# Loads for a half's end issued during its last gate and up block, and VectorE adds to y in the last row line

## The chip, the cores and the metric

The kernel runs on one core of one Trainium2 chip. The metric is device time in microseconds of one execution, as the median over runs. The engines of the core are TensorE (PE; its weight loads stand apart as PEld), VectorE (DVE), ScalarE (ACT), GpSimd (POOL) and SyncE (SP), and 16 DMA engines that move data between HBM and the on-chip memory. SP issues nearly all loads, in the order of its queue; POOL issues the few transfers that add while they move.

## What is computed

One layer of a hybrid encoder on 256 tokens of width 2048, in float32. It is a feed-forward half step, a mixing stage (attention and a Fourier branch), and another feed-forward half step:

```python
def _swiglu(x, w_gate, w_up, w_down):
    return (jax.nn.silu(x @ w_gate) * (x @ w_up)) @ w_down

def _macaron_ffn(x, pre_g, w_gate, w_up, w_down, post_g):
    return x + MACARON_WEIGHT * _rms_norm(_swiglu(_rms_norm(x, pre_g), w_gate, w_up, w_down), post_g)
...
        h = _macaron_ffn(h, ffn1_pre_g[l], ffn1_w_gate[l], ffn1_w_up[l], ffn1_w_down[l], ffn1_post_g[l])
        h = _gated_mixers(h, mix_pre_g[l], w_in[l], b_gate[l], q_norm_g[l], k_norm_g[l],
                          w_attn_o[l], w_fourier[l], w_out[l], mix_post_g[l], rope)
        h = _macaron_ffn(h, ffn2_pre_g[l], ffn2_w_gate[l], ffn2_w_up[l], ffn2_w_down[l], ffn2_post_g[l])
```

The hidden width of a feed-forward half is 5632. The change touches the two feed-forward halves alone.

## The kernel before

**Number format.** Each float32 factor is split into a high part (line 104, ScalarE) and a low part (line 105, VectorE), and a product is three matmuls: high by high, high by low, low by high (lines 110 to 112). TensorE's work is therefore fixed by the shapes, and every weight that is loaded costs one ScalarE and one VectorE instruction before TensorE can use it.

**A half (`ffn`, line 703).** The hidden width is cut into 11 blocks of 512. For each block, gate and up products are formed (a 2048-deep sum), silu and multiplication give the block of hidden values, these are transposed on TensorE, and the block's rows of the down matrix are multiplied and added to `y`, which has 256 tokens (two tiles of 128, `t` = 0 and 1) by 2048 columns (four column blocks `cb` of 512). The first two gate and up blocks are done plainly; the nine that follow run through a software pipeline:

- `swiglu` (line 558) is one gate and up block. Its depth is cut into eight pairs of 128-deep pieces. Pairs 0, 1, 2, 4, 5 and 6 use a seven-product scheme (`seven`, 21 matmuls a pair), pairs 3 and 7 the plain one (`plain`, 24 matmuls a pair). For the scheme VectorE first forms sums of weights (line 582). Even pairs load 1 MB at once (`raw4`), the others 512 KB pieces (`raw`).
- `row_line` (line 658) is one row block of the down product: four column blocks of 24 matmuls, with two weight pieces each. At the start of its last column block (`ahead`) the next block's hidden values are transposed.
- `Line` (line 525) is the queue that holds both together: a step's weights are loaded and split when it is fed, and its matmuls come when it is popped, up to `RING` = 6 steps later, or 8 (`RING + RING_B8`) where `turn["more"]` is set. With `turn["more"]` every fourth split goes into a place of the pool `b8` (line 512) and not into the ring.
- The steps' order on TensorE, ScalarE and VectorE is the order of the code (`manual_schedule`, line 735). The order on SP and POOL, and of what stands outside such a section, is a planner's, which works with modelled times.

The loop at line 736 runs f from 2 to 11; its f-th turn does row block f - 2, then gate and up block f. So in the order of TensorE the last gate and up block (f = 10) is followed by row block 9 (f = 11), and row block 10 follows in `last_rows`.

**The pool `b8`** has 12 places of 1 MB. In the pipeline two hold `y`; six hold the *left factors*: the normalized input in the forms that the two schemes need, made once a half (`Forms`, line 443) and put into three rooms of two places each, in the order of the pairs. The first room holds pairs 0, 1 and the first two forms of pair 2, the second the rest of pair 2 and pairs 3 and 4, the third pairs 5, 6 and half of pair 7. The other four places turn over among `raw4` and the splits of `turn["more"]`.

**How y is added up.** Of each row block, column blocks 2 and 3 (`onto`) start from y: ScalarE copies y into PSUM (line 681), TensorE adds on top, ScalarE copies back (line 691). Column blocks 0 and 1 start from zero: ScalarE copies the result into a buffer `part` (line 694), and a DMA issued from POOL adds that to y while it moves it (line 695).

**The end of a half (`last_rows`, line 261).** Row block 10 runs token tile by token tile. For each, ScalarE first copies y's column block into PSUM (`row_part`, line 219), TensorE adds the product, and the squares for the norm (line 379) and the rest of the norm follow. This needs `h` (the residual, two places of b8, 1 MB a tile) and the norms' gains as broadcast rows (`gpost`, and in the first half `gpre` for the stage behind it; 1 MB each). `tail` loads them: line 795 for the first half, where h is the input x, and line 1225 for the second, where it comes from a spill in DRAM and there is only one gain. It is called when TensorE's order reaches column block 1 of row block 9 (line 744), though SP may issue the loads whenever their places are free.

Of the kernel before, what the change touches and what calls it, by code (L numbers as in the profile page):

```python
# [15 lines left out]
ALU = mybir.AluOpType  # L16
# [33 lines left out]
PLAIN = 2  # L50
# [8 lines left out]
def encoder_layer(  # L59
# [495 lines left out]
            while self.queue:  # L555
                self.next()

    def swiglu(line, forms, w, hs):


        ps, begun, x = {}, set(), {}

        def mul(n, a, b, last=False):
            if n not in ps:
                ps[n] = ptr.tile([P, NB], F32, tag="tr", name="pc") if n in ("p5", "p7", "p1") else                     pmm.tile([P, NB], F32, tag="mm", name="pc")
            mm3(ps[n][:], *a, *b, n not in begun, last)
            begun.add(n)

        def raw(pair, i):
            return raw_piece(w[pair // 2], pair % 2 * 2 + i)  # L570

        def plain(pair, i, *then, hold=False):
            def use(b):
                for t in range(NT):
                    for j in range(2):
                        k = 2 * pair + j
                        mul("gu"[i] + str(t), forms.plain[k][t], b[j], k == KD - 1)

            line.feed(lambda: ring(raw(pair, i)[:]), use, *then, hold=hold)

        def minus(out, a, b):
            V.tensor_tensor(out=out, in0=a, in1=b, op=ALU.subtract)  # L582

        def add(out, a, b):
            if out not in x:
                x[out] = work(out)
            V.tensor_tensor(out=x[out][:], in0=ps[a][:], in1=x[b][:], op=ALU.add)

        def copy():
            x["x1"] = work("x1")  # L590
            A.activation(x["x1"][:], ps["p1"][:], AF.Copy)

        def silu(t):
            g = x["x" + "13"[t]]
            A.activation(g[:], g[:], AF.Silu)

        def times(t):
            g, up = x["x" + "13"[t]], x["x" + "25"[t]]
            V.tensor_tensor(out=up[:], in0=up[:], in1=g[:], op=ALU.mult)
            hs.append(up)  # L600

        def seven(pair, between=None, *then):
            a11, a12, na22, s1, s2, s3, s4 = forms.seven[pair]
            end = pair == BY_SEVEN[-1]
            h = {}

            def first():
                t = chunk.tile([P, WP, NB], F32, tag=("ch_hi", "ch_lo")[BY_SEVEN.index(pair) % 2], name="t13")
                if turn["more"] and pair in RAW_B8:
                    four = big("raw4", F32, [P, 2 * WP, NB])  # L610
                    load(four[:], w[pair // 2].rearrange("p (i k c) -> p i k c", i=2, c=NB)[:, pair % 2])
                    ra, rb = four[:, 0:WP, :], four[:, WP:, :]
                    minus(t[:], four[:, 1:3, :], ra)
                else:
                    ra, rb = raw(pair, 0), raw(pair, 1)
                    minus(t[:, 0, :], ra[:, 1, :], ra[:, 0, :])
                    minus(t[:, 1, :], rb[:, 0, :], ra[:, 1, :])
                h.update(ra=ra, rb=rb, t=t)
                b = ring(rb[:])
                minus(ra[:, 1, :], rb[:, 0, :], t[:, 0, :])  # L620
                return b

            def second():
                b = ring(h["t"][:])
                minus(h["t"][:, 0, :], h["ra"][:, 1, :], h["rb"][:, 1, :])
                return b

            def two(n, a, m, b, last):
                def use(ws):
                    mul(n, a, ws[0], last)  # L630
                    mul(m, b, ws[1], last)
                return use

            line.feed(first, two("u0", s4, "g0", a12, False))
            line.feed(second, two("p5", s1, "p7", s3, end), hold=end)
            if between:
                between()
            line.feed(lambda: ring(h["ra"][:]), two("p1", a11, "p6", s2, end), *then[0:2], hold=end)
            line.feed(lambda: ring(h["t"][:, 0:1, :]), lambda ws: mul("g1", na22, ws[0]), *then[2:], hold=end)

        sums = [copy, lambda: add("x2", "p6", "x1"), lambda: add("x3", "p7", "x2"), lambda: add("x2", "p5", "x2"),
                lambda: add("x5", "p5", "x3")]
        gates = [lambda: add("x1", "g0", "x1"), lambda: add("x3", "g1", "x3"), lambda: silu(0), lambda: silu(1)]
        ups = [lambda: add("x2", "u0", "x2"), lambda: times(0), lambda: add("x5", "u1", "x5"), lambda: times(1)]
        for kg in range(KD // CK):
            a, b = 2 * kg, 2 * kg + 1
            if kg == KD // CK - 1:
                seven(a, None, *sums)
                plain(b, 0, *gates, hold=True)
                plain(b, 1, *ups)  # L650
            elif b in BY_SEVEN:
                seven(a)
                seven(b)
            else:
                seven(a, lambda: plain(b, 0))
                plain(b, 1)

    def row_line(line, ch, w, rb, y, first, ahead):

        rooms = {(0, 0): (ptr, "tr"), (1, 0): (ptr, "tr"), (1, 1): (ptr, "tr")} if not first else {}
        ps = {}

        def onto(cb):
            return cb >= ONTO and not first

        def place(cb, t):
            pool, tag = rooms.get((cb, t), (pmm, "mm"))
            ps[cb, t] = pool.tile([P, NB], F32, tag=tag, name="pr")  # L670

        def use(b, cb, i):
            if i == 0 and cb in ahead:
                ahead[cb]()
            for t in range(NT):
                if i == 0 and not onto(cb):
                    place(cb, t)
            if i == 1 and cb + 2 < D // NB and onto(cb + 2):
                for t in range(NT):
                    place(cb + 2, t)  # L680
                    A.activation(ps[cb + 2, t][:], cbs(y[t], cb + 2), AF.Copy)
            for t in range(NT):
                for j in range(WP):
                    k = i * WP + j
                    mm3(ps[cb, t][:], ch[0][:, k, t * P:(t + 1) * P], ch[1][:, k, t * P:(t + 1) * P], *b[j],
                        k == 0 and not onto(cb), k == CK - 1, onto(cb))

        def out(t, cb):
            dst = cbs(y[t], cb)
            if first or onto(cb):  # L690
                A.activation(dst, ps[cb, t][:], AF.Copy)
            else:
                part = work("part")
                A.activation(part[:], ps[cb, t][:], AF.Copy)
                nc.gpsimd.dma_start(dst, part[:], accum_op=ALU.add)

        for cb in range(D // NB):
            for i in range(CK // WP):
                line.feed(lambda i=i, cb=cb: ring(raw_piece(w[rb, cb], i)[:]),
                          lambda b, cb=cb, i=i: use(b, cb, i),  # L700
                          *([lambda t=t, cb=cb: out(t, cb) for t in range(NT)] if i == CK // WP - 1 else []))

    def ffn(u, rs, wg, wu, wgu, wd, yname, tail, gate0, w_next=None, early=()):
# [31 lines left out]
        with tc.manual_schedule(engines={mybir.EngineType.DVE, mybir.EngineType.Activation, mybir.EngineType.PE}):  # L735
            for f in range(PLAIN, nblk + 1):

                def ahead(hs=hs, f=f):
                    chs.append(new_chunk("hT")) if f > PLAIN else None
                    turn_h(chs[-1], hs)  # L740

                before = {D // NB - 1: ahead}
                if f == nblk:
                    before[1] = lambda: end.extend(tail(y))
                if f == PLAIN:
                    before[0] = lambda: forms.chunk(KD // CK - 1)
                turn["more"] = PLAIN <= f - 1 < nblk - 1
                row_line(line, chs[-1] if f > PLAIN else chs[0], wd, f - 2, y, f == PLAIN, before)
                if f < nblk:
                    hs = []  # L750
                    turn["more"] = True
                    swiglu(line, forms, wgu[f - PLAIN], hs)
            line.end()
        norm, nxt = end
        return last_rows(chs[-1], wd, nblk - 1, y, norm, nxt, w_next), nxt
# [39 lines left out]
    def tail(y):  # L795
        for t in range(NT):
            h[t] = big(f"h{t}")
            load(h[t][:], x[t * P:(t + 1) * P, :])
        g_post, g_pre = bcast(f1_post, "gpost1"), bcast(mix_pre, "gpre1")
        return PostNorm(y, h, g_post, 0.5), NextInput(y, h, g_pre)  # L800

    pk, nxt = ffn(u, rs, f1_gate, f1_up, f1_gu, f1_down, "y", tail, gate0, w_in[4],
                  early=[lambda t=t: root_of_x(t) for t in range(NT)])
# [421 lines left out]
    def tail(y):  # L1225
        for t in range(NT):
            h3[t] = big(f"h3{t}")
            load(h3[t][:], spill2[t])
        return PostNorm(y, h3, bcast(f2_post, "gpost3"), 0.5, store), None

    ffn(nxt.u, nxt.rs, f2_gate, f2_up, f2_gu, f2_down, "yf", tail, lambda: pg, early=[finish])

# [140 lines left out]
```

## Time and profile before

| what | us |
|---|---|
| median of 3 runs | 2016.39 |
| lowest and highest run | 2015.51, 2016.53 |
| the profiled execution | 2016.2 |
| its span, first to last instruction | 2014.4 |
| TensorE busy in it | 1987.2 |
| VectorE busy in it | 1776.3 |
| ScalarE busy in it | 1304.9 |

The rows of the profile are read like this. Times are from the start of the span. In a timeline a row is start, duration, engine, line, operation, what it writes and reads, shape, and in brackets how long the engine stood idle before it and which instruction ended that. Names carry no buffer numbers: `pr` is a PSUM tile of a row block, `pc` of a gate, up or other column block, `raw` a loaded weight piece, `whi`, `wlo`, `wh`, `wl` and `w` its split parts, `hTh` and `hTl` the transposed hidden values, `pt` a transpose's result. A duration of a matmul overlaps with the next one's, so the steps between their starts tell TensorE's pace. A "stretch" is a window of time with each engine's busy time and count of instructions in the order PE, PEld, DVE, ACT, POOL, then the granted TensorE clock (1.00 is full), the busy share of the DMA engines and their GB/s.

The first half ends at about 710 us, the second with the span.

### The profile page before, as it was taken

Reading aid. Unit: us, or ns where it says so; the run is one execution under the profiler, and the core shown is the slowest. Engines: PE = TensorE matmul, PEld = TensorE weight load, DVE = VectorE, ACT = ScalarE, POOL = GpSimd, SP = SyncE. Lnnn points to the kernel's source line nnn. Section 1 sums busy time; section 2 is a strip of 40 time slices with the busy share of each in tenths; the row PEclk is TensorE's granted clock in tenths of the full one; section 3 lists DMA queues with packets and bytes.
Section 4 is the critical chain, followed back from the end, with each engine's and each line's share of the span. In section 5 each row is a group of like instructions: output and inputs, shape, how many; then the busy total and the mean of one; then the engine's idle time right before and its main releaser. Section 6 shows DMA issues by size and latency. Waiting matters only on the chain.

```text
span 2014.4 us, 25830 instructions
## 1 busy us (share of the span) xinstructions
PE 1987.2 (99%) x9146; PEld 1645.6 (82%) x9146; DVE 1776.3 (88%) x2344; ACT 1304.9 (65%) x1868; POOL 91.6 (5%) x102
## 2 busy tenths in 40 slices
PE   9999999999999899999999999999999999999997
PEld 7888888888888778888888888878888888888886
DVE  6999999999999678886878886778999999999995
ACT  7566766667766756556676564645677766667666
POOL 0000000000000010100000000000000000000002
PEclk9999999999999999999999999999999999999999
DMA  8647776677767796964555657566577766677674
GB/s 319 213 169 250 222 231 198 203 237 239 222 206 239 252 297 194 258 199 145 188 186 175 203 171 274 190 215 196 173 237 230 228 211 211 207 234 227 217 246 153
DMA packets 118738, 436.31 MB, mean 217 GB/s; under 512 B 12968, under 2 KB 19120, under 8 KB 107216
## 3 DMA queue, kind: packets, MB, share of 16 engines
q1 hardware_dynamic: 103888, 411.65, 60.3%
q0 software_dynamic: 14720, 23.01, 6.6%
q8 instruction: 71, 1.16, 0.2%
q14 instruction: 59, 0.48, 0.1%
HBM read 409.44 MB, written 6.29 MB: 206 GB/s over the span
## 4 chain that ended last, share of the span: by engine, by line
PE 61%; issue 29%; DMA 6%; DVE 3%; ACT 1%; POOL 0%; SPq 0%; DVEq 0%; POOLq 0%; ACTq 0%
PE pc L111 12%; PE pc L112 12%; PE pc L110 12%; PE pr L111 7%; PE pr L110 7%; PE pr L112 7%; DMA yf<-part 4%; DVE wlo L105 1%; PE pt L180 1%; DMA raw<-in_w_fo 1%; DMA draw<-in_dft_pos 0%; ACT whi L104 0%; DMA raw<-in_f_down 0%; PE pe L110 0%; PE pe L112 0%
## 5 line engine op out<-in xcount | busy, mean ns | idle before, releaser
L105 DVE TENSOR_TENSOR wlo<-raw,whi 128x1024 fp32r<-128x1024 f32 (+1 forms) x571 | 684.9, 1218 | 107.8 <-ACT whi L104 106.5
L104 ACT ACTIVATE whi<-raw 128x1024 fp32r<-128x1024 f32 (+1 forms) x571 | 589.6, 1053 | 251.7 <-PE pc L112 108.8
L112 PE MATMUL pc<-whi,fl 128*128 128x512 f32 x738 | 287.3, 389 | 0.0
L111 PE MATMUL pc<-wlo,fh 128*128 128x512 f32 x738 | 287.2, 389 | 0.0
L110 PE MATMUL pc<-whi,fh 128*128 128x512 f32 x738 | 287.1, 389 | 0.0
L110 PE MATMUL pc<-whi,uh 128*128 128x512 f32 x688 | 271.9, 395 | 1.1 <-ACT uh L779 1.1
L111 PE MATMUL pc<-wlo,uh 128*128 128x512 f32 x688 | 270.1, 393 | 1.0 <-DVE wlo L105 1.0
L112 PE MATMUL pc<-whi,ul 128*128 128x512 f32 x688 | 269.9, 393 | 0.0
L104 ACT ACTIVATE whi<-t 128x1024 fp32r<-128x1024 f32 (+1 forms) x198 | 171.6, 866 | 138.2 <-DVE t L582 127.8
L110 PE MATMUL pr<-whi,hTh 128*128 128x512 f32 x560 | 220.8, 394 | 7.4 <-ACT pr L219 6.3
L111 PE MATMUL pr<-wlo,hTh 128*128 128x512 f32 x560 | 219.0, 391 | 0.4 <-DVE wlo L105 0.4
L582 DVE TENSOR_TENSOR t<-raw 128x512 f32<-128x512 f32 (+1 forms) x252 | 208.8, 840 | 11.6 <-DMA raw<-in_f_gu 7.8
L112 PE MATMUL pr<-whi,hTl 128*128 128x512 f32 x560 | 218.8, 391 | 0.0
L105 DVE TENSOR_TENSOR wlo<-t,whi 128x1024 fp32r<-128x1024 f32 (+1 forms) x198 | 193.3, 976 | 13.2 <-ACT whi L104 12.7
L104 ACT ACTIVATE w<-raw 128x1024 fp32r<-128x1024 f32 x140 | 147.8, 1056 | 41.9 <-DVE raw L582 34.7
L105 DVE TENSOR_TENSOR w<-raw,w 128x1024 fp32r<-128x1024 f32 x140 | 170.5, 1218 | 0.0
L111 PEld LDWEIGHTS pc<-wlo,fh 128*128 128x128 f32 x738 | 138.5, 188 | 29.0
L110 PEld LDWEIGHTS pc<-whi,fh 128*128 128x128 f32 x738 | 138.5, 188 | 28.9
L112 PEld LDWEIGHTS pc<-whi,fl 128*128 128x128 f32 x738 | 138.5, 188 | 28.8
L110 PEld LDWEIGHTS pc<-whi,uh 128*128 128x128 f32 x688 | 129.8, 189 | 28.2 <-ACT uh L779 2.5
L111 PEld LDWEIGHTS pc<-wlo,uh 128*128 128x128 f32 x688 | 129.7, 189 | 28.0 <-DVE wlo L105 3.1
L112 PEld LDWEIGHTS pc<-whi,ul 128*128 128x128 f32 x688 | 129.8, 189 | 27.0
(358 smaller groups left out, 3175.2 us busy)
## 6 DMA issues: line engine op xcount, KB each, us to landing
raw<-in_f_down SPq DMA_DIRECT2D x176, 512.0 KB, 5.1
raw<-in_f_gu SPq DMA_DIRECT2D x144, 512.0 KB, 4.7
raw<-in_f_gu SPq DMA_DIRECT2D x72, 1024.0 KB, 6.8
raw<-in_w_in SPq DMA_DIRECT2D x112, 512.0 KB, 4.8
raw<-in_f_up SPq DMA_DIRECT2D x32, 512.0 KB, 4.3
raw<-in_w_ao SPq DMA_DIRECT2D x32, 512.0 KB, 4.0
raw<-in_w_out SPq DMA_DIRECT2D x32, 512.0 KB, 4.4
raw<-in_f_gate SPq DMA_DIRECT2D x31, 512.0 KB, 5.3
```

The source lines that it names most:

```text
L104: a = A.activation(hi, src, AF.Copy)
L105: v = V.tensor_tensor(out=lo, in0=src, in1=hi.bitcast(F32), op=ALU.subtract)
L110: T.matmul(ps, lh, rh, start=first, stop=False, skip_group_check=onto)
L111: T.matmul(ps, lh, rl, start=False, stop=False, skip_group_check=onto)
L112: return T.matmul(ps, ll, rh, start=False, stop=last, skip_group_check=onto)
L180: T.transpose(pt[:, j, :], src[:, j * P:(j + 1) * P], ident[:])
L582: V.tensor_tensor(out=out, in0=a, in1=b, op=ALU.subtract)
```

## The change

`tail` is cut in two and called from the last gate and up block. `swiglu` takes a dictionary `behind`: what stands there for a pair is called when that pair's steps have been fed. For f = 10 the loads of h are called behind pair 5 and those of the gains behind pair 6. At that point the code has popped the steps of pairs 0 to 3, and of 0 to 4 respectively, so that the first and then the second room of left factors has no reader left to come.

In the last row line (f = 11) column blocks 0 and 1 go "add": VectorE adds PSUM to y in one instruction, in place of ScalarE's copy and POOL's adding DMA. The other row lines keep the DMA ("dma"), and the first (f = 2) still sets y ("set"). `turn["more"]` is now set for f = 11 too, so the last row line queues 8 steps deep and puts every fourth split into b8.

```diff
-    def swiglu(line, forms, w, hs):
+    def swiglu(line, forms, w, hs, behind={}):
...
                 seven(a, None, *sums)
+                if a in behind:
+                    behind[a]()
                 plain(b, 0, *gates, hold=True)
...
                 seven(b)
+                if b in behind:
+                    behind[b]()
...
-    def row_line(line, ch, w, rb, y, first, ahead):
+    def row_line(line, ch, w, rb, y, way, ahead):
+        first = way == "set"
...
             if first or onto(cb):
                 A.activation(dst, ps[cb, t][:], AF.Copy)
+            elif way == "add":
+                V.tensor_tensor(out=dst, in0=ps[cb, t][:], in1=dst, op=ALU.add)
             else:
                 part = work("part")
...
                 before = {D // NB - 1: ahead}
-                if f == nblk:
-                    before[1] = lambda: end.extend(tail(y))
...
-                turn["more"] = PLAIN <= f - 1 < nblk - 1
-                row_line(line, chs[-1] if f > PLAIN else chs[0], wd, f - 2, y, f == PLAIN, before)
+                turn["more"] = f > PLAIN
+                way = "set" if f == PLAIN else "dma" if f < nblk else "add"
+                row_line(line, chs[-1] if f > PLAIN else chs[0], wd, f - 2, y, way, before)
                 if f < nblk:
                     hs = []
                     turn["more"] = True
-                    swiglu(line, forms, wgu[f - PLAIN], hs)
+                    swiglu(line, forms, wgu[f - PLAIN], hs, {
+                        5: lambda: end.append(tail(y)), 6: lambda: end.extend(end.pop()())} if f == nblk - 1 else {})
...
     def tail(y):
         for t in range(NT):
             h[t] = big(f"h{t}")
             load(h[t][:], x[t * P:(t + 1) * P, :])
-        g_post, g_pre = bcast(f1_post, "gpost1"), bcast(mix_pre, "gpre1")
-        return PostNorm(y, h, g_post, 0.5), NextInput(y, h, g_pre)
+        def gains():
+            g_post, g_pre = bcast(f1_post, "gpost1"), bcast(mix_pre, "gpre1")
+            return PostNorm(y, h, g_post, 0.5), NextInput(y, h, g_pre)
+
+        return gains
...
-        return PostNorm(y, h3, bcast(f2_post, "gpost3"), 0.5, store), None
+        return lambda: (PostNorm(y, h3, bcast(f2_post, "gpost3"), 0.5, store), None)
```

## The prediction

> **What bounds the kernel now.** I read the page first, then TensorE's waits, then the timeline of each engine around the ends of the two feed-forward halves, then the DMA shares in stretches of 4 us.
>
> ```profile
> span 2014.4 us, 25830 instructions
> ...
> PE 1987.2 (99%) x9146; PEld 1645.6 (82%) x9146; DVE 1776.3 (88%) x2344; ACT 1304.9 (65%) x1868; POOL 91.6 (5%) x102
> ```
>
> TensorE is busy for 1987.2 of 2014.4 us. The change takes no matmul away, so it can only give back idle time of TensorE, and slow matmuls that follow idle time: 27 us at most. The waits say where that time is (total, times, longest):
>
> ```profile
> PE pr L110 <- ACT pr L219: 6.3, 2, 6.0
> PE pt L180 <- DVE y L418: 3.4, 1, 3.4
> ```
>
> No row of the steady loop stands there: the waits that matter belong to the ends. The first lies at the end of the first half, between the last row line and `last_rows`:
>
> ```profile
> 670.95 1.03 PE L180 MATMUL pt<-ident,x 128*128 128x128 f32 x8
> ...
> 677.66 0.50 PE L110 MATMUL pr<-whi,hTh 128*128 128x512 f32 x1 [0.22 <-ACT pr L219]
> 678.00 0.40 PE L111 MATMUL pr<-wlo,hTh 128*128 128x512 f32 x1
> ...
> 680.29 0.39 PE L112 MATMUL pr<-whi,hTl 128*128 128x512 f32 x1
> 686.71 0.80 PE L110 MATMUL pr<-whi,hTh 128*128 128x512 f32 x1 [6.03 <-ACT pr L219]
> 687.30 0.63 PE L111 MATMUL pr<-wlo,hTh 128*128 128x512 f32 x1
> ...
> 689.86 0.63 PE L111 MATMUL pr<-wlo,hTh 128*128 128x512 f32 x1
> ```
>
> From 678.00 to 680.29 lie ten matmuls: 0.229 us each. Then TensorE waits 6.03 us, and the seven steps from 686.71 to 689.86 take 3.15 us where seven at 0.229 are 1.60: 1.55 us more. With the 0.22 at 677.66 this end loses **7.80 us**. TensorE waits for line 219, ScalarE's copy of y into PSUM. What ScalarE did instead:
>
> ```profile
> 677.54 0.58 ACT L691 ACTIVATE y<-pr 128x512 f32<-128x512 f32 x1
> 681.21 1.06 ACT L104 ACTIVATE wh<-raw 128x1024 fp32r<-128x1024 f32 x1 [3.08 <-DMA raw<-in_f_down]
> ...
> 684.54 0.59 ACT L379 ACTIVATE junk<-pr 128x512 f32<-128x512 f32 x1
> ...
> 686.06 0.60 ACT L219 ACTIVATE pr<-y 128x512 f32<-128x512 f32 x1
> ```
>
> It stood 3.08 us for a weight load, and had that split, other splits and the squares of line 379 queued ahead of the copy. The chain of waits names that load, and the DMA queues (packets, MB, share of 16 engines) over 672 to 685 say what it shared the engines with:
>
> ```profile
> 673.26 7.92 DMA raw<-in_f_down
> ```
>
> ```profile
> q0 software_dynamic: 352, 0.62, 28.4%
> ```
>
> The load took 7.92 us. 28.4% of 13 us is 3.7 us of all 16 engines, spent on the accumulating transfers of line 695 (issued from POOL) that add `part` to y. In the stretches (the last two columns are DMA share and GB/s) the engines are full then, but nearly empty shortly before the loads of h come:
>
> ```profile
> 636.00:640.00 4.00, 4.00 (x19) 3.33 (x18) 3.97 (x6) 2.65 (x3) 0.00 (x0) 1.00 0.20 61
> ...
> 644.00:648.00 4.00, 4.00 (x19) 3.32 (x18) 4.00 (x5) 3.54 (x5) 0.00 (x0) 1.00 1.00 417
> ...
> 676.00:680.00 4.00, 3.78 (x17) 2.82 (x16) 2.00 (x2) 2.06 (x3) 0.00 (x0) 1.00 1.04 341
> ```
>
> At the second half's end the wait is for the accumulating transfer itself:
>
> ```profile
> 1980.15 0.60 ACT L219 ACTIVATE pr<-yf 128x512 f32<-128x512 f32 x1 [4.09 <-DMA yf<-part]
> ```
>
> ```profile
> 1981.80 0.50 PE L110 MATMUL pr<-whi,hTh 128*128 128x512 f32 x1 [1.20 <-ACT hTh L104]
> ...
> 1989.77 0.50 PE L111 MATMUL pr<-wlo,hTh 128*128 128x512 f32 x1 [0.38 <-DVE wlo L105]
> ```
>
> ScalarE's order holds line 219 ahead of the split of hT, so 4.09 us of waiting there become 1.20 us on TensorE; with the 0.38 this end loses **1.58 us**.
>
> **The change part by part.**
>
> *The adds.* In the last row line (row block 9) the column blocks 0 and 1 of both token tiles take "add": four ScalarE copies and four accumulating transfers go in each half, four VectorE adds of 128x512 from PSUM come. The nearest row is VectorE's other operation on such a pair:
>
> ```profile
> L384 DVE TENSOR_TENSOR y<-pr,gpost x8: 682/691/693, 686.0 to 709.1; 128x512 f32<-128x512 f32 x8
> ```
>
> Four by 0.69 is 2.8 us of VectorE a half. An add waits for TensorE's end of its column block; behind it in VectorE's order stand the splits of hT and of row block 10. The stretch 676 to 680 has VectorE busy for 2.00 of 4 us, and the pieces of row block 9 are all split ahead of the adds, since the queue then holds all eight. I take 0; were the cover gone it would be 2.8 a half. What it removes: y of these blocks is final one add after TensorE, not one transfer after it, so line 219 for row (0,1) depends on nothing slow and has no reason to stand behind the squares. Also 3.7 us of DMA time between 672 and 685 are given to the weight loads. At the second half's end the 4.09 us go with the transfer they waited for, and the 1.58 with them.
>
> *The loads.* TensorE's program order gives times: before the transposes at 670.95 lie 72 matmuls of the row line, 24 of the last gate and up pair (7) and 21 of pair 6, 117 by 0.229 is 26.8, so pair 6 begins at 644.2, pair 5 (21) at 639.4, and pair 2 ended at 631.8 (21 of pair 4 and the last 12 of pair 3 earlier). The first room of left factors (pairs 0, 1, part of 2) is free from 631.8, the second (to pair 4) from 639.4. SP's issues:
>
> ```profile
> 630.53 0.33 SPq L85 DMA_DIRECT2D raw<-in_f_gu  x1
> ...
> 639.42 0.90 SPq L85 DMA_DIRECT2D h<-in_x  x2
> ```
>
> The two loads of h can so begin about 7.6 us sooner, in the stretch where the DMA share was 0.20, and the gains from about 639 on. That is 4.2 MB in the first half, 3.1 in the second, off the full stretch. At 417 GB/s h and gains are some 10 us of DMA time; together with the 3.7 above this is more than the 6.03 us that the late load cost. I count the first end's 7.80 us as gone. What is late next there: the copies of line 219 have ScalarE's own splits as the only rival (below).
>
> *What the loads are moved past.* On SP's queue they now precede the 1 MB load of pair 6, issued at 630.53. VectorE takes it up at 639.53, and its last use for a double split ends at 645.48:
>
> ```profile
> 639.53 1.22 DVE L582 TENSOR_TENSOR t<-raw 128x1024 f32<-128x1024 f32 x1
> ...
> 644.26 1.22 DVE L105 TENSOR_TENSOR w<-raw,w 128x1024 fp32r<-128x1024 f32 x1
> ```
>
> TensorE needs that third step after twelve matmuls of pair 6, at 644.2 + 2.7 = 646.9: it has 1.5 us in hand. The share of 0.20 from 636 to 640 says that pair 6's load was through by about 636.8 (0.8 us of traffic), so VectorE has 2.7 in hand. Both h loads ahead are 2.1 MB: 5.0 us at 417 GB/s, 6.2 at 341. Late on TensorE by at most 5.0 - 2.7 - 1.5 = 0.8, or 2.0, a half; by nothing if pair 6's load goes first. I take 0, since the engines stood idle there and a part of the two loads runs beside the issue; 2.0 a half stays in the range. VectorE, busy 3.97 of 4 us, can't catch up before the row line.
>
> The Trainium skill bears on this ("DMA: Bandwidth & Descriptors", Specifications): it puts a core's share of HBM at about 358 GB/s, by which 2.1 MB would need an estimated 5.9 us and pair 6 would come 0.9 us later than I count. The 417 GB/s of this case's row, while h was loaded, stands against that, and the measurement is used.
>
> *The ring.* With `more` kept on, the last row line splits two of eight pieces into b8 places and queues eight deep. b8 has twelve: y, h and the gains six, two of row weights, the third room and the places of raw loads make it up without a wait in the order of the code; earlier row lines run in just this form and no wait of theirs stands in the list. 0.
>
> The sum, against the profiled execution: 2016.2 (span 2014.4 and 1.8 around it) - 7.80 - 1.58 = **2006.8 us**. The median of the runs shown is 2016.39, 0.2 above.
>
> **The rivals.**
>
> *ScalarE's order stays.* If line 219 for row (0,1) still stands behind the squares, these can't start before TensorE's row (0,0) ends at 680.52. From the squares' start at 684.54 to the copy's end at 686.66 passed 2.1 us, so 2.1 of the 6.03 remain: 2008.9; with the slow matmuls again 2010.5. For it: that order is in the trace. Against it: what made the copy late (the transfer into y) is gone. The Trainium skill ("TensorE: Matmul & The Clock Gate", Part 1: The HAM clock gate) says that an idle window of some 3.4 us halves the clock; by that rule 2.1 us would cost no clock and 2008.9 holds. The rows agree as far as they go: 0.63 us matmuls follow the 6.03, and 0.40 the 0.22.
>
> *The loads are late anyway.* If what fills the engines from 652 on is the weights themselves, or h still comes late because its places aren't given sooner, the first end keeps its 7.80: 2014.6. For it: 341 GB/s at a share of 1.04 with no h under way. Against it: the 28.4%.
>
> *The 3.4 us wait for line 418 goes too.* It lies behind the first end, where the planner places VectorE's order; shifted times may move it. 3.4 and as many slow matmuls (1.55) less: 2001.8. Nothing in the change touches it.
>
> *Slower: SP stands.* If a load of h is given a place of the second room, it blocks SP's queue until 639.4, with pair 6's load behind it: 8.9 us later, plus one load of 2.5, less 2.7 and 1.5 in hand, is a wait of 7.2, and 1.55 of slow matmuls, 8.75 a half. Both halves: 17.5 - 9.4 = 8.1 more, **2024.3**. It decides from 4.7 a half on. Against it: the first room is free earlier, and one place is enough for one load.
>
> **How the numbers follow.** Forecast 2006.8: 0.50, its own range 2005 to 2011 (2.0 a half on the upper side). Order stays: 0.14. Loads late: 0.15. Wait for line 418 gone: 0.12. Slower: 0.09. The range holds all but the last and some edges: 2001.5 to 2015.0. 0.2% (4 us, about what a measurement of this kernel can tell from no change) puts the bounds at 2012.4 and 2020.4: faster 0.50 + 0.14 + 0.12 less an edge, 0.74; within 0.15 and that edge, 0.17; slower 0.09.
>
> **What would show it.** Right: the accumulating transfers fall by four a half; h is issued near 632 and the gains near 640; the row of 6.3 us for line 219 goes from TensorE's waits; no wait of ScalarE for `yf<-part` at the second end; TensorE has no wait inside the last gate and up block. Wrong: a wait of TensorE or VectorE in pair 6 (the slower case), a wait of about 2 us for line 219 (the order), 6 us again for `raw<-in_f_down` (the loads), or a wait of the same size at another line of `last_rows`, which I have no row for.

## The result, and the profile after

| | median us | lowest to highest | runs |
|---|---|---|---|
| before | 2016.53 | 2015.51 to 2018.33 | 5 |
| after | 2006.3 | 2002.77 to 2009.31 | 5 |

The ratio is 0.9948, with a 95% interval of 0.9933 to 0.9962: 10.2 us less. The profiled execution of the changed kernel took 2006.3 us as well. The head of its page:

```profile
span 2004.2 us, 25805 instructions
...
PE 1984.0 (99%) x9146; PEld 1644.8 (82%) x9146; DVE 1780.1 (89%) x2352; ACT 1301.2 (65%) x1860; POOL 84.5 (4%) x94
...
q0 software_dynamic: 13568, 20.91, 6.0%
```

TensorE has the same 9146 matmuls in a span that is 10.2 us shorter. VectorE has eight instructions more, ScalarE eight fewer, and q0, the queue of the transfers that add (packets, MB, share of 16 engines), moves 2.1 MB less: four transfers of 256 KB a half. TensorE's waits now begin like this (total, times, longest):

```profile
PE pt L180 <- DVE y L418: 2.5, 1, 2.5
PE pc L111 <- DVE wlo L105: 1.7, 4, 0.7
```

No row of line 219 is left, and none of a row block (`pr`) at all. ScalarE's timeline at the first half's end says why (line 691 is now 696, and 681 is 686):

```profile
667.90 0.58 ACT L219 ACTIVATE pr<-y 128x512 f32<-128x512 f32 x1
...
670.88 0.60 ACT L219 ACTIVATE pr<-y 128x512 f32<-128x512 f32 x1
...
674.75 0.61 ACT L219 ACTIVATE pr<-y 128x512 f32<-128x512 f32 x1
676.24 1.06 ACT L104 ACTIVATE wh<-raw 128x1024 fp32r<-128x1024 f32 x1 [0.88 <-DMA raw<-in_f_down]
...
682.67 0.58 ACT L379 ACTIVATE junk<-pr 128x512 f32<-128x512 f32 x1
...
683.24 0.59 ACT L219 ACTIVATE pr<-y 128x512 f32<-128x512 f32 x1
```

Before the change the second copy of line 219 stood behind the squares of line 379 and began at 686.06. Now three copies are done before the first square. The four adds that they rest on are VectorE's:

```profile
665.19 2.48 DVE L698 TENSOR_TENSOR y<-pr,y 128x512 f32<-128x512 f32 x4
```

The loads moved as the code says. SP's queue:

```profile
630.80 0.80 SPq L85 DMA_DIRECT2D h<-in_x  x2
632.38 0.33 SPq L85 DMA_DIRECT2D raw<-in_f_gu  x1
...
640.14 0.38 SPq L85 DMA_DIRECT2D gpost<-in_f_post  x1
640.61 0.38 SPq L85 DMA_DIRECT2D gpre<-in_mix_pre  x1
```

To compare kernels, the table below adds up TensorE's loss in their traces: over every step from the start of one matmul of lines 110 to 112 to the next start on TensorE, what lies above 0.229 us (steps under 0.33 left out). So it holds the waits and the slow matmuls behind them. "First end" is 655 to 705 us, "second end" from 1950 us on. These two columns, in us, come from one traced execution of each kernel, which need not be the one with the median time.

| kernel | median us | ratio to before [95%] | first end | second end |
|---|---|---|---|---|
| before | 2016.53 | 1 | 8.54 | 2.38 |
| after | 2006.3 | 0.9948 [0.9933, 0.9962] | 0.00 | 0.00 |
| e1, adds alone | 2005.63 | 0.9942 [0.9930, 0.9954] | 0.51 | 0.00 |
| e2, early loads alone | 2016.65 | 0.9993 [0.9982, 1.0003] | 5.87 | 4.72 |
| e3, deeper queue alone | 2017.21 | 1.0001 [0.9992, 1.0010] | 7.00 | 4.34 |
| e4, all but the deeper queue | 2007.02 | 0.9958 [0.9944, 0.9972] | 1.11 | 1.28 |
| e5, gains behind pair 5 too | 2013.74 | 0.9977 [0.9968, 0.9986] | 0.00 | 0.00 |
| e6, e1, copies and transfers | 2016.62 | 1.0001 [0.9992, 1.0009] | 8.35 | 2.31 |
| e7, after, constants first | 2005.11 | 0.9944 [0.9930, 0.9957] | 0.57 | 0.00 |
| e8, after, constants early | 2002.61 | 0.9932 [0.9919, 0.9944] | 0.37 | 0.00 |
| e9, e1 and transfers only | 2008.65 | 0.9959 [0.9946, 0.9971] | 2.87 | 0.87 |
| e10, e1, constants early | 2003.51 | 0.9932 [0.9918, 0.9945] | 0.11 | 0.11 |
| e11, e1 and copies only | 2013.40 | 0.9979 [0.9970, 0.9988] | 5.36 | 0.59 |
| e12, before, ScalarE's order | 2013.54 | 0.9987 [0.9978, 0.9996] | 3.84 | 5.07 |

The two ends lost 8.54 + 2.38 = 10.9 us and lose nothing now: as much as the whole gain. Each ratio is against runs of the kernel before that went with it on the same chip (medians 2016.34 to 2017.35).

### The profile page after: what moved, and what is told of

Read it like the earlier page. It is cut to its first block, busy times and chain, and to the rows that moved or that the text cites. A ratio compares the mean times of both kernels' runs of the same rounds, so it can differ in the third digit from the quotient of the medians.

```text
span 2004.2 us, 25805 instructions
## 1 busy us (share of the span) xinstructions
PE 1984.0 (99%) x9146; PEld 1644.8 (82%) x9146; DVE 1780.1 (89%) x2352; ACT 1301.2 (65%) x1860; POOL 84.5 (4%) x94
## 4 chain that ended last, share of the span: by engine, by line
PE 90%; DVE 5%; DMA 3%; ACT 1%; issue 1%; SPq 0%; DVEq 0%; ACTq 0%
PE pc L111 18%; PE pc L112 18%; PE pc L110 18%; PE pr L112 10%; PE pr L111 10%; PE pr L110 10%; DVE wlo L105 2%; PE pt L180 1%; DMA raw<-in_f_gu 1%; DMA raw<-in_w_fo 1%; DVE t L582 0%; PE pe L110 0%; PE pe L112 0%; PE pe L111 0%; PE pt L1072 0%
## 5 line engine op out<-in xcount | busy, mean ns | idle before, releaser
L110 PE MATMUL pr<-whi,hTh 128*128 128x512 f32 x544 | 213.4, 392 | 0.0
L112 PE MATMUL pr<-whi,hTl 128*128 128x512 f32 x544 | 211.8, 389 | 0.0
L111 PE MATMUL pr<-wlo,hTh 128*128 128x512 f32 x544 | 211.7, 389 | 0.0
L104 ACT ACTIVATE w<-raw 128x1024 fp32r<-128x1024 f32 x144 | 152.0, 1055 | 40.8 <-DVE raw L582 34.7
L105 DVE TENSOR_TENSOR w<-raw,w 128x1024 fp32r<-128x1024 f32 x144 | 175.6, 1219 | 0.0
```

The source lines that it names most:

```text
L104: a = A.activation(hi, src, AF.Copy)
L105: v = V.tensor_tensor(out=lo, in0=src, in1=hi.bitcast(F32), op=ALU.subtract)
L110: T.matmul(ps, lh, rh, start=first, stop=False, skip_group_check=onto)
L111: T.matmul(ps, lh, rl, start=False, stop=False, skip_group_check=onto)
L112: return T.matmul(ps, ll, rh, start=False, stop=last, skip_group_check=onto)
```

## The experiments

**The change in its three parts.** The account of the prediction is that the adds and the early loads win the time together. Its rivals: the adds alone, the loads alone, the deeper queue. e1 is the kernel before with the adds only:

```diff
+            elif way == "add":
+                V.tensor_tensor(out=dst, in0=ps[cb, t][:], in1=dst, op=ALU.add)
```

> The adds alone: VectorE adds in the last row line, h and the gains are loaded where they were before, and the queue of the last row line is six deep as before. Theory A (transfers that add to y hold up the weight loads and the copies of line 219): most of the gain is here, 2007 to 2009.5, with no wait for line 219 over 1 us at either end. Theory B (h and the gains fill the DMA engines in the last row line): the second end's 1.6 to 2.4 us go, the first end keeps most of its 8, 2013 to 2015.

It measured 2005.63 us: the whole gain, without a load moved, and below the ranges of both theories. Its waits have no row of line 219 either.

e2 has the early loads only (`tail` cut in two and called behind pairs 5 and 6, row block 9 as before).

> The early loads alone: h behind pair 5, gains behind pair 6, y still added to by transfers, queue six deep as before. Theory A: the weights are less late, but line 219 still waits for a transfer: first end 3 to 6 us lost instead of 8.4, the second end about as before, 2011 to 2015. Theory B: the first end's loss goes, 2007.5 to 2010, the second end about as before.

2016.65 us, no gain that can be told from nothing, and above the ranges of both theories. In its trace the first end loses less than before the change (5.87 us for 8.54), but the second more (4.72 for 2.38). The copies of line 219 stand early in ScalarE's order here, but wait for the transfers into y, ahead of the split of hT:

```profile
672.55 0.60 ACT L219 ACTIVATE pr<-y 128x512 f32<-128x512 f32 x1 [1.16 <-DMA y<-part]
...
677.55 0.60 ACT L219 ACTIVATE pr<-y 128x512 f32<-128x512 f32 x1 [3.89 <-DMA y<-part]
```

So the old way of adding costs at either place: behind the squares the copy is late, ahead of them it waits for the transfer.

e3 has the deeper queue only, e4 everything but the deeper queue. This line of the change is the one that e3 takes and e4 leaves out:

```diff
-                turn["more"] = PLAIN <= f - 1 < nblk - 1
+                turn["more"] = f > PLAIN
```

> The deeper queue alone: eight steps and every fourth split in b8 in the last row line, loads and adding transfers as before. Both theories: no change, 2014.5 to 2018. Theory C (weights that are split earlier are what removes the first end's wait): 2008 to 2011.

> The change without the deeper queue: early loads and VectorE's adds, six steps deep as before. Theories A and B: as the whole change, 2004 to 2008.5. Theory C: 2012 to 2016.

2017.21 and 2007.02 us: the deeper queue brings nothing alone, and nothing that can be measured within the whole (e4's interval and that of after overlap). The traces hint at a use for it all the same. At the start of the last row line, around 657 us and again at 1950 to 1960, e4 loses 1.11 and 1.28 us behind the split of a weight (line 105), and e2, which also joins early loads to a queue six deep, 0.93 and 0.85. e1, six deep with the old loads, loses 0.51 us there and nothing in the second half; e3 and the changed kernel, eight deep, lose nothing at all. So the early loads seem to cost a little there, which the deeper queue covers; by the medians neither is shown.

**The slower rival.** e5 is the changed kernel with the gains called behind pair 5 too, so ahead of pair 6's load on SP:

```diff
-                        5: lambda: end.append(tail(y)), 6: lambda: end.extend(end.pop()())} if f == nblk - 1 else {})
+                        5: lambda: end.extend(tail(y)())} if f == nblk - 1 else {})
```

> The changed kernel with the gains' loads moved from behind pair 6 to behind pair 5, so that SP has h and the gains ahead of pair 6's 1 MB load. If the prediction's slower case is priced right (SP stands until the second room is free, near 639.4 us, and the gains' loads run ahead of pair 6): pair 6's load comes 9 us later plus 5 us for two gains in the first half, 2.5 for one in the second, less 4.2 in hand, and 1.55 of slow matmuls after each wait: 11 and 9 us more, 2022 to 2028. Rival (places of the ring come free sooner, or the queue absorbs it): 2005 to 2011.

SP's queue, VectorE and TensorE:

```profile
633.14 0.33 SPq L85 DMA_DIRECT2D gpre<-in_mix_pre  x1
639.15 0.33 SPq L85 DMA_DIRECT2D raw<-in_f_gu  x1
```

```profile
645.79 1.22 DVE L582 TENSOR_TENSOR t<-raw 128x1024 f32<-128x1024 f32 x1 [5.54 <-DMA raw<-in_f_gu]
```

```profile
646.98 0.51 PE L110 MATMUL pc<-whi,fh 128*128 128x512 f32 x1 [2.42 <-ACT whi L104]
648.24 0.56 PE L111 MATMUL pc<-wlo,fh 128*128 128x512 f32 x1 [0.76 <-DVE wlo L105]
```

SP issues nothing for 6 us, until about when the prediction has the second room free (639.4). Pair 6's load goes out at 639.15 where it went at 632.38, VectorE stands 5.54 us for it, and TensorE waits. In the gate and up blocks TensorE loses 5.30 us in the first half and 2.33 in the second, where there is one gain only; in the changed kernel it loses nothing there. These 7.6 us are of the size of the difference of the medians, 7.4 (2013.74 - 2006.3), and of the ratios, 5.8 (0.9977 - 0.9948, times 2017). So the danger is real, at less than half of the expected price (20 us, for 11 and 9), and the order in which the change issues its loads escapes it.

**What the adds take away.** e6 puts what the adds removed back beside them: e1, a ScalarE copy of each PSUM block, and an adding transfer of it into a scratch tile. The edit makes each add wait for its copy.

```diff
-                V.tensor_tensor(out=dst, in0=ps[cb, t][:], in1=dst, op=ALU.add)
+                scr = work("scr")
+                nc.gpsimd.memset(scr[:], 0.0)
+                part = work("part")
+                c = A.activation(part[:], ps[cb, t][:], AF.Copy)
+                v = V.tensor_tensor(out=dst, in0=ps[cb, t][:], in1=dst, op=ALU.add)
...
+                nc.gpsimd.dma_start(scr[:], part[:], accum_op=ALU.add)
```

> The adds alone, as in the run with VectorE's adds and the old loads, but ScalarE's copies and the four adding transfers of the last row line are kept in each half, into a scratch tile that nothing reads (POOL clears it first). Theory A1 (the transfers' share of the DMA engines makes the weights late): most of the loss comes back, 2012 to 2017. Theory A2 (what counts is that line 219 waits for y's own transfer): 2004 to 2008, with no wait for line 219 over 1 us.

2016.62 us: all of the gain is lost. But this does not show that the DMA time did it. With the copies back, line 219's second copy stands behind the squares again, and ScalarE once waited for a work tile that a transfer still held:

```profile
671.85 0.60 ACT L701 ACTIVATE part<-pr 128x512 f32<-128x512 f32 x1 [2.44 <-DMA scr<-part]
...
683.64 0.58 ACT L379 ACTIVATE junk<-pr 128x512 f32<-128x512 f32 x1
...
685.44 0.58 ACT L219 ACTIVATE pr<-y 128x512 f32<-128x512 f32 x1
```

Two theories are left: the loss is the transfers' DMA time (A1 below), or the copies' place and waits in ScalarE's order (A2). e9 and e11 take them apart. e9 has e1's adds and four transfers a half from y into a scratch room of `b8`; ScalarE makes no copy and waits for none. e11 has e1's adds, but each reads a copy that ScalarE makes; there is no transfer.

```diff
                 V.tensor_tensor(out=dst, in0=ps[cb, t][:], in1=dst, op=ALU.add)
+                if not ps.get("scr"):
+                    ps["scr"] = big("scr")
+                    nc.gpsimd.memset(ps["scr"][:], 0.0)
+                i = 2 * cb + t
+                nc.gpsimd.dma_start(ps["scr"][:, i * NB:(i + 1) * NB], dst, accum_op=ALU.add)
```

```diff
-                V.tensor_tensor(out=dst, in0=ps[cb, t][:], in1=dst, op=ALU.add)
+                part = work("part")
+                A.activation(part[:], ps[cb, t][:], AF.Copy)
+                V.tensor_tensor(out=dst, in0=part[:], in1=dst, op=ALU.add)
```

> The adds alone (old loads, old queue), and behind each of them an accumulating transfer of 256 KB from y into a scratch room of b8, four a half: the transfers' DMA time is back, and ScalarE makes no copy for them and waits for none of them. Theory A1 (the transfers' DMA time made the loss): a PE wait of 4 us or more at the copies into PSUM is back at 680-690 and the time is 2012 to 2017. Theory A2 (what the adds took away is the copies' place and waits in ScalarE's order, not the DMA time): no such wait, time 2004 to 2008.

> The adds alone, but each reads a copy in SBUF that ScalarE makes of the sum, as before the change: four copies a half are back on ScalarE, and no transfer. A1 (the transfers' DMA time): no PE wait at 680-690, time 2004 to 2008. A2 (the copies on ScalarE and the order that they bring): ScalarE's copies into PSUM come behind the squares again, PE waits for them, time 2012 to 2017.

e9 over 672 to 685 us (the queues; then ScalarE's and TensorE's timelines):

```profile
q1 hardware_dynamic: 833, 3.04, 62.1%
q0 software_dynamic: 467, 0.84, 37.0%
```

```profile
676.74 1.10 ACT L219 ACTIVATE pr<-y 128x512 f32<-128x512 f32 x2
...
682.30 1.06 ACT L104 ACTIVATE wh<-raw 128x1024 fp32r<-128x1024 f32 x1 [3.94 <-DMA raw<-in_f_down]
```

```profile
686.11 0.50 PE L111 MATMUL pr<-wlo,hTh 128*128 128x512 f32 x1 [0.56 <-DVE wlo L105]
...
688.76 0.50 PE L110 MATMUL pr<-wh,hTh 128*128 128x512 f32 x1 [1.20 <-ACT pr L219]
```

The transfers have more of the engines than in the kernel before (37.0%, where it was 28.4%), the weight load costs ScalarE 3.94 us of standing against 3.08, and yet the first end loses 2.87 us and not 8.54: here the copies stand ahead of that load's split. Its 2008.65 us lie just above A2's range and far below A1's. e11, without a transfer:

```profile
676.08 0.65 ACT L219 ACTIVATE pr<-y 128x512 f32<-128x512 f32 x1
...
681.30 0.58 ACT L379 ACTIVATE junk<-pr 128x512 f32<-128x512 f32 x1
...
683.27 0.58 ACT L219 ACTIVATE pr<-y 128x512 f32<-128x512 f32 x1
```

```profile
683.91 0.79 PE L110 MATMUL pr<-whi,hTh 128*128 128x512 f32 x1 [3.50 <-ACT pr L219]
```

y was ready in time (the adds were done by 670.4), no adding transfer was under way, and TensorE waited 3.50 us for a copy that stands behind the squares. The share of the DMA engines over 672 to 685 is 1.00 in e9 and 0.80 in e11, and yet e11 is the slower one. By the ratios e9 costs 3.4 us against e1 (0.9959 - 0.9942, times 2017), e11 7.5, and e6, with both, 11.9, each uncertain by 3 to 3.5 us, so that e9's loss is hardly told from nothing. By the two columns of the table e9 costs 3.2 us (3.74 - 0.51) and e11 5.4. At the second end neither brings the 2.38 us back (0.87 and 0.59): what the kernel before waits for there is the landing of the transfer into `yf` itself (4.09 us on ScalarE, as the prediction's row shows). So, by these runs, the larger part of the gain is that ScalarE no longer copies, and that the copies of line 219 stand early for it; the transfers' DMA time is the smaller and less certain part. e11's profiled execution, 2008.47 us, was the fastest of its eleven: what its median lost beyond the table was not seen. Nor is it known what in the planner's model puts the copies behind the squares.

e12 asks the kernel before for the order alone: all copies and transfers stay, and only the first half's end is traced so that the copies for column blocks 0 to 2 of token tile 0 stand ahead of the squares and of the splits of row block 10's later weight pieces.

```diff
+            for cb in range(3):
+                p = pmm.tile([P, NB], F32, tag="mm", name="pr")
+                held.append((p, A.activation(p[:], cbs(y[0], cb), AF.Copy)))
+            with tc.issue_after(held[1][1].ins):
+                ws += [weights(w[rb, cb], spare=SPARE[cb]) for cb in range(2, D // NB)]
...
+                with tc.issue_after(held[2][1].ins):
+                    norm.block(0, cb, p)
```

> The kernel before with all its ScalarE copies and accumulating transfers, and its loads where they were. Only ScalarE's order at the first half's end is changed: the copies of y into PSUM for column blocks 0, 1 and 2 of token tile 0 stand ahead of the splits of row block 10's later pieces and ahead of the squares. Theory A2 (that order was the loss, the transfers were not): TensorE's 6 us wait goes at the first end, the second end (some 2 us) stays, time 2008 to 2011. Theory A1 (the transfers' DMA time was the loss): the pieces still come late, TensorE waits 4 us or more for them or for the copies at 680-690, time 2013 to 2018.

ScalarE and TensorE (lines 273 and 222 are the copies of line 219):

```profile
674.56 0.62 ACT L273 ACTIVATE pr<-y 128x512 f32<-128x512 f32 x1
677.11 0.60 ACT L273 ACTIVATE pr<-y 128x512 f32<-128x512 f32 x1 [1.93 <-DMA y<-part]
```

```profile
685.15 0.39 PE L112 MATMUL pr<-whi,hTl 128*128 128x512 f32 x1
687.61 0.66 PE L110 MATMUL pr<-wh,hTh 128*128 128x512 f32 x1 [2.07 <-ACT pr L222]
688.07 0.63 PE L111 MATMUL pr<-wl,hTh 128*128 128x512 f32 x1
...
691.05 0.47 PE L112 MATMUL pr<-wh,hTl 128*128 128x512 f32 x1
```

The wait of 6.03 us is gone with every transfer in place. A shorter one has come, for the copy of the fourth column block, which the edit left behind the second square. At the first end 4.7 us are won, but at the second, which the edit did not touch, 2.7 are lost: ScalarE waits 4.99 us for the transfer into `yf`, and TensorE 2.96 for the split behind it. The median, 2013.54, falls into A1's range, though A1's sign, a wait of 4 us or more at 680 to 690, isn't there: the second end holds it up. So the order alone, all transfers in place, is worth more than half of the first end's loss in this trace; why the untouched second end got worse is open.

**The next stall.** In the changed kernel the largest stall left lies around the wait for line 418: 5.0 us at 705 to 735, with the slow matmuls. ScalarE stands there for constants of the mixing stage:

```profile
712.75 0.42 ACT L104 ACTIVATE dps<-draw 128x258 fp32r<-128x258 f32 x1 [8.35 <-DMA draw<-in_dft_pos]
```

e7 traces the constants ahead of the spill of h; e8 loads four of the six in the first half's first gate and up block; e10 is e8 without early loads and deeper queue (e1 with those constants). The line by which e8 and e10 call the code that they move:

```diff
-                  early=[lambda t=t: root_of_x(t) for t in range(NT)])
+                  early=[lambda t=t: root_of_x(t) for t in range(NT)] + [constants])
```

> The changed kernel with the mixing stage's constants traced ahead of the spill of h and of the rope tables. Their loads are issued some 4 us sooner. If the remaining wait of TensorE for line 418 (2.5 us and slow matmuls after it, 5.4 us in all from 700 to 730) comes from the constants' landing: 2001 to 2005. If it comes from the DMA engines being full of the spill and the weights of f: no change, 2004 to 2008.

> The changed kernel with four of the six constants loaded and split during the first half's first block, so that no split of a constant stands between the norm's steps at the first half's end. If the wait for line 418 comes from them: it goes, 2000 to 2004. If something else takes its place there, or the first block loses as much: 2004 to 2008.

> The adds alone, with four of the six constants of the spectral part loaded and split in the first half's first gate and up block. If the early loads of the change bring nothing beside the adds, 2001 to 2004 as with the whole change and these constants (2002.61); if they bring something that the constants laid bare, 2005 or more.

e7 (2005.11 us) only exchanges the wait for another, since the split of `dps` now stands ahead of a weight's on VectorE (its traced execution, 2008.61 us, was the slowest of its five):

```profile
714.28 0.80 PE L111 MATMUL pc<-wlo,uh 128*128 128x512 f32 x1 [3.85 <-DVE wlo L105]
```

e8 loses 3.6 us in that stretch, not 5.0, and is the fastest median here, 2002.61; its interval still touches that of after. e10 has the same ratio, 0.9932: with this stall reduced, too, the early loads bring nothing that can be measured.

## Why the prediction was right, and where its reasons were not

The forecast was 2006.8 us and the median came out at 2006.3. Its terms, one by one:

- **The two ends.** Predicted as 7.80 and 1.58 us, both to go in full. By the table's count they were 8.54 and 2.38, and both went. Each was sized some 0.8 us too small: the times in brackets were added as they stand, where the step of a wait lost about 0.16 us more each time, and of the slower steps behind a wait only seven were counted, all of the first end.
- **The adds at no cost.** Right. Four take 2.48 us of VectorE at 665.19, and TensorE waits for nothing behind them. The reason given for the copies, that y is final one add after TensorE and line 219 "has no reason to stand behind the squares", is what after, e1 and e9 show. e11 adds that an early y isn't enough: with ScalarE's copies back, the old order is back. The 3.7 us of DMA time that the prediction set beside this reason count for less: e9 has them back and keeps most of the gain.
- **The early loads.** This step was wrong. The prediction set "some 10 us of DMA time", taken off the full stretch, beside the transfers' 3.7, and weighed the two together against 6.03. e2 shows that the loads alone bring nothing, and e1 that nothing is missing without them. The traffic did move (in after: duration; busy time and count of PE, PEld, DVE, ACT and POOL; granted clock, DMA share, GB/s):

```profile
636.00:640.00 4.00, 4.00 (x19) 3.30 (x19) 3.97 (x6) 1.81 (x3) 0.00 (x0) 1.00 0.98 415
```

  The share of 0.20 at 636 has become 0.98. Over 672 to 685 it was 0.92 before the change, and e1, with the old loads, has 0.79:

```profile
672.00:685.00 13.00, 8.45 (x36) 6.32 (x35) 8.49 (x9) 9.19 (x13) 0.00 (x0) 0.95 0.92 287
```

```profile
672.00:685.00 13.00, 13.00 (x61) 10.81 (x60) 10.18 (x11) 11.64 (x19) 0.00 (x0) 1.00 0.79 264
```

  The early loads alone (e2) bring it to 0.80, and the whole change has 0.85. So either part relieves that stretch about as much, and only the adds gain time: what failed is the step that counted relief of the DMA engines there as TensorE's time. That the total came out right all the same is luck in this part, since the adds alone carry what had been credited to both.
- **Pair 6's load behind h.** Right at 0: it went out at 632.38 behind both loads of h, VectorE stood 0.30 us for it, and TensorE not at all.
- **The deeper queue at 0.** Right as far as the medians tell (e3, e4); the traces hint at up to 2.4 us beside early loads.
- **ScalarE's order stays** (2008.9, or 2010.5 with slow matmuls). Not what the change does, but e11 is that case: the rival left 2.1 us of the wait, and 3.50 were there. e11's median of 2013.4 holds more than that, which was not seen.
- **The loads are late anyway** (2014.6). A stretch full without a load of h under way is what e9 has (1.00), and its time is 2008.65: late loads cost little once the copies stand ahead of them.
- **The wait for line 418.** It stayed, 2.5 us where it was 3.4.
- **Slower: SP stands.** It did not happen, but e5 shows the mechanism, at 5.30 and 2.33 us against the 8.75 a half that were worked out. What stood was pair 6's own load, not a load of h.

## What to carry to other kernels

Where an engine waits long for a short instruction, look at what stands ahead of that instruction on its own engine before looking at what that engine waited for: the late weight load in ScalarE's row was real, but by these runs the copy's place behind it cost more than the load. A transfer that adds while it moves makes its result late for whoever reads it next, so the last sum before a dependent stage is better added by an engine, while the others can keep the DMA. And a change of several parts that gives the time foretold has not shown that all of its parts do anything: one run of each part alone told that here.

## What the runs showed of the hardware that was not expected

TensorE's matmuls became slow after shorter waits than assumed. In e12 a wait of 2.07 us was followed by steps of 0.43 us from 688.07 to 691.05, and the granted clock (the column ahead of the DMA share) fell:

```profile
688.00:692.00 4.00, 4.00 (x12) 3.13 (x11) 2.98 (x6) 3.23 (x7) 0.00 (x0) 0.60 0.96 385
```

After e9's wait of 1.20 us the steps stayed at 0.23, but for the first. Nor is a wait of some 2 us always followed by slow matmuls: in e11 TensorE waits 2.23 us for line 418 until 718.73, and from 720.11 on the steps are 0.23 us and the granted clock 1.00. The Trainium skill ("TensorE: Matmul & The Clock Gate", Part 1: The HAM clock gate) has the clock halve after an idle window of about 3.4 us. The prediction used that rule to say that a wait of 2.1 us costs no clock. The measurement decides: in e12 the eight steps from 687.61 to 691.05 took 3.44 us where eight at 0.229 take 1.83, so 1.6 us came on top of the 2.07.
